# Levels of a chunked recurrence: keys and queries in one row, and three visits to TensorE instead of one per level

## The chip, the cores and the metric

The kernel runs on one core of a Trainium2 chip. The metric is the device time of one execution in microseconds (us). Names of engines as in the profile: PE is TensorE (PEld its weight loads), DVE is VectorE, ACT is ScalarE, POOL is GpSimd, SP is SyncE.

## What is computed

One layer of a hybrid decoder for 2048 prompt tokens and 64 sample tokens (8 sequences of 8), model width 1024. A projection of the normalised input gives nine parts of 1024 columns. Three of them (q, f, v) feed a recurrence with 8 heads of 128 x 128 state; the others feed a convolution branch and gates. Cut to the recurrence, which the change touches:

```python
f = lb + (1.0 - lb) * jax.nn.sigmoid(fz)
k = 1.0 - f
# per token: S_t = diag(f_t) S_{t-1} + (1 - f_t) i_t^T ; o_t = S_t^T q_t, done in chunks:
b = jnp.cumsum(log_f, axis=-2)
decay = jnp.exp(jnp.where(mask, b[..., :, None, :] - b[..., None, :, :], -jnp.inf))
attn = jnp.einsum('bhtk,bhsk,bhtsk->bhts', qc, kc, decay)
o = einsum(attn, v) + einsum(q * exp(b), S)
```

Everything else (projection, gates, convolution, layer norm, output projections) is the same before and after the change.

## The kernel before

**Phases.** The first and longest phase, to about 1960 us, is the projection. It goes over two halves of the tokens (1024 each; the second half also holds the 64 sample tokens) and, in each, over 8 heads. For a head, nine blocks of weights (f, q, v, za, zb, gb, ga, ma, mb) meet each stretch of tokens. One block times one stretch is a *unit*: 24 matmuls into one PSUM bank (line 1356; high and low parts of weights and activations, 8 steps of the contraction, 3 products). A unit of 512 tokens counts as 1.0 on the planner's clock. The first half has units of 512 tokens; the second has 512, 256 and 320. After the projection come the two branch products with the layer norm, and then the output projections (line 1187).

**What hangs between the units.** Everything else of the phase is put into a list with a due time (`at_time`), and the main loop (lines 1338 to 1364) emits, after the 24 matmuls of a unit, all steps whose due time falls into it, in order of priority and time, and then the unit's evacuation. So on PE the small matmuls of the recurrence stand between two units, together with any others due in the same unit. On the page I call such a gap a *visit*. Each engine executes its own list in order.

**The recurrence.** `Hgrn` handles one head and one stretch of 512 tokens (the last stretch also the 64 sample tokens): 8 heads x 4 stretches = 32 instances. The causal 128 x 128 products are built in levels h = 1, 2, 4, 8, 16, 32, 64. At level h, tokens are taken in blocks of 2h; the queries of the second half of a block meet the keys of the first half. `decay(h)` (DVE, line 429) multiplies keys and queries by the running decay and writes them to a level tile; `grow(h)` (line 419) doubles the running decay; `mm_level(h)` (PE, lines 455 and 463) does the products; `mm_diag` (line 441) does the diagonal. Up to level 16 the weights are 32 tokens wide, the output goes to four groups of 32 partitions, and a mask keeps what belongs to the level; level 32 also uses weights of 32 columns, level 64 of 64. All other matmuls of the phase (projection, transposes, `mm_kv`, `mm_o`) use weights of 128 columns. The diagonal and levels 1 to 8 go to the PSUM tile `d32p`, 16 to 64 to `ab`. DVE takes the diagonal and levels 1 to 16 out by `evac_diag` and `evac_level` (lines 470, 479), `final` (line 500) scales keys and queries to the stretch's end, ACT's `gather` copies the blocks into `at`, and `k_turn`, `mm_kv`, `chain`, `mm_o`, `norm_o` and `turn_o` finish.

**The level tiles.** There are three, `lvl[0]` to `lvl[2]`, of two rows of 576. A level uses one tile: row 0 for keys, row 1 for queries, each only at the positions of its half blocks. Level h uses tile `h.bit_length() % 3`, so that a tile comes again every third level.

**Due times.** `plan` (line 614) gives each step its time after the start of the instance. Before the change, decay and grow of the i-th level are due at 0.75 i, its matmuls 1.25 units later (`MMD`), that is at 1.25, 2.0, 2.75, 3.5, 4.25, 5.0 and 5.75; the diagonal at 1.25. The second instance of a head starts 6.1 units or more after the first.

Of the kernel before, what the change touches and what calls it, by code (L numbers as in the profile page):

```python
# [17 lines left out]
P = 128  # L18
# [11 lines left out]
RAW_LAG = 1  # L30
KTS = 7.7
SIN = 1.0
MMD = 1.25
VEC_AT = 6
FILL_PRIO = 0
LNT = (-0.4, 2, 2.6, 4, 5, 8, 8.1, 9.6, 9.1, 10.5)
# [38 lines left out]
def view(t, off, dims):  # L75
    return bass.AP(t.tensor, t.offset + off, [list(t.ap[0])] + [list(d) for d in dims])
# [7 lines left out]
def tile_hybrid_step(  # L84
# [201 lines left out]
    lvl = [c1.tile([P, 2, 576], F32, name=f"lvl{i}") for i in range(3)]  # L286
# [62 lines left out]
    def at_time(t, fn, prio=2):  # L349
        todo.append((t, prio, len(todo), fn))  # L350


    s_state = {}

    class Hgrn:


# [61 lines left out]
            nc.vector.tensor_tensor(out=io, in0=io, in1=tt, op=ALU.mult)  # L419

        def decay(self, h):
            n = self.n if h <= 4 else 512
            nb = n // (2 * h)
            lv = lvl[h.bit_length() % 3]
            if h == 1:
                o, a, b = (view(t, 577, [[2, n // 2]]) for t in (lv, self.kq, self.rp))
            else:
                o, a, b = (view(t, 0, [[576 + h, 2], [2 * h, nb], [1, h]]) for t in (lv, self.kq, self.rp))
            nc.vector.tensor_tensor(out=o, in0=a, in1=b, op=ALU.mult)  # L429

        def chunks(self, h):
# [11 lines left out]
                        start=True, stop=True)  # L443

        def mm_level(self, h):
            lv = lvl[h.bit_length() % 3]
            kk = self.kq if h == 1 else lv
            if h == 16:
                self.ab = ps_1.tile([P, 4, P], F32, tag="ab", name="ab")
            if h <= 16:  # L450
                dst, s = (self.ab, 0) if h == 16 else (d32p, 16 + 16 * h.bit_length())
                for c, nq in self.chunks(h):
                    for b in range(nq):
                        o = P * c + 32 * b
                        nc.tensor.matmul(  # L455
                            dst[32 * b:32 * b + 32, c, s:s + 16], lhsT=kk[:, 0, o:o + 32],
                            rhs=lv[:, 1, o:o + 32].rearrange("p (a e i) -> p a e i", e=2, i=h)[:, :, 1, :],
                            start=True, stop=True)
            else:
                for c in range(4):  # L460
                    for b in range(64 // h):
                        o = 2 * h * b
                        nc.tensor.matmul(
                            self.ab[o:o + h, c, o + h:o + 2 * h], lhsT=lv[:, 0, P * c + o:P * c + o + h],
                            rhs=lv[:, 1, P * c + o + h:P * c + o + 2 * h], start=True, stop=True)

        def evac_diag(self):
            m = self.m
# [145 lines left out]
        def plan(self, t0, tv):  # L614

            smp = self.smp
            ev = []

            def put(t, *fns):
                for fn in fns:  # L620
                    at_time(t0 + t, fn, 0)

            put(0.0, self.prep)
            put(MMD, self.mm_diag)
            for i, h in enumerate((1, 2, 4, 8, 16, 32, 64)):
                put(0.75 * i, lambda h=h: self.decay(h), lambda h=h: self.grow(h))
                put(0.75 * i + MMD, lambda h=h: self.mm_level(h))
            put(3.2, self.evac_diag, lambda: self.evac_level(1), lambda: self.evac_level(2))
            put(4.5, lambda: self.evac_level(4), lambda: self.evac_level(8))
            put(5.25, self.final)  # L630
            put(4.6 + MMD, lambda: self.evac_level(16))
            put(6.25, self.k_turn)
            put(6.6, self.gather)
            put(7.25, self.mm_kv)
            put(8.2, self.chain)
            put(9.0, self.mm_o)
            put(9.9, self.norm_o)
            put(11.2, self.turn_o)
            if smp:
                put(KTS, self.k_turn_sample)  # L640
                put(7.5, self.sample_o)
                put(8.3, self.sample_norm)
                put(9.5, self.sample_turn)
                put(8.0, self.sample_decay)
                put(9.2, lambda: self.sample_state(0))
                put(9.9, lambda: self.sample_state(1))
            at_time(tv, self.v_turn)
            if self.smp:
                at_time(tv + 1.0, self.v_turn_sample)
# [263 lines left out]
    for which, w, times, ev in (("a", w_br_a, t_a, evac_a), ("b", w_br_b, t_b, evac_b)):  # L913
        for hf in range(2):
# [3 lines left out]
            for dms in ((0, 1), (2,), (3,), (4,), (5,), (6, 7)):  # L918
                bs = [Block(w[0][:, P * dm:P * (dm + 1)]) for dm in dms]
                for s in range(2):  # L920
                    for dm, b in zip(dms, bs):
                        for _, t0, c0, n in (p for p in parts if p[0] == s):
                            pre, e = ev(dm, t0, n)
# [142 lines left out]
    for i in range(9):  # L1066
        t, b = XOUT0 + XOUT_STEP * i, 8 + i
# [255 lines left out]
    for t, prio, n, fn in todo:  # L1323
        i = min(bisect.bisect_right(clock, t + 1e-6) - 1, len(units) - 1)
# [5 lines left out]
    for b in range(1, len(blocks)):  # L1330
        i = 1 if b == 2 else max(uses[b][0] - 3, 0)
        if b >= 3:
            i = max(i, min(uses[b - 3][-1] + 1, uses[b][0] - 1))
# [4 lines left out]
    for i, u in enumerate(units):  # L1338
# [13 lines left out]
        for k in range(KB):  # L1352
            for fn in u.mid.get(k, []):
                fn()
            for w, x in ((u.block.hi, xh), (u.block.hi, xl), (u.block.lo, xh)):
                nc.tensor.matmul(  # L1356
                    ps[:, 0:u.n], lhsT=w[:, k, :], rhs=x[:, k, sl],
                    start=(k == 0 and w is u.block.hi and x is xh), stop=(k == KB - 1 and w is u.block.lo))
# [106 lines left out]
```

## Time and profile before

| what | value |
|---|---|
| median of 3 runs | 2814.08 us (2813.54 to 2814.91) |
| the profiled execution | 2815.03 us, of which the profile's span is 2813.2 |
| mean granted clock of PE | 0.996 |
| PE, PEld, DVE, ACT, POOL busy | 2781.4, 2378.6, 1934.6, 932.1, 278.6 us |
| narrow matmuls of the levels (lines 441, 455, 463), records | 1056, 5216, 768 |
| DVE's taps of the convolution (line 696) | 722.4 us in 960 instructions |

A row of a timeline has the start in us from the span's start, the length in us, the engine, the source line, the operation, output<-inputs by the program's names, shapes, and how many alike were merged; behind it, in brackets, the idle time of the engine ahead of it and what ended it. For a matmul the first shape is that of the weights ("128*32": 128 rows, 32 columns), the second that of what streams. Every matmul in plain 32 bits leaves two records; those of the projection leave one. A row of waits reads: engine, what waited <- what for: us in total, number of times, longest. A row of stretches has the stretch, its length, busy us and instructions (x) of PE, PEld, DVE, ACT and POOL, the granted clock, the share of the DMA engines and GB/s. A row of groups ends in busy us, mean ns of one | idle us ahead of it and what ended that.

### The profile page before, as it was taken

What the parts mean: (1) busy time and instruction counts of PE and PEld (TensorE: products, weight loads), DVE (VectorE), ACT (ScalarE), POOL (GpSimd) and SP (SyncE); (2) the same over time, 40 slices, a digit from 0 to 9 for tenths busy, and PEclk for the clock granted to TensorE, in tenths of its full rate; (3) what the DMA queues carried; (4) which work ended last, traced back from release to release, by engine and by line L of the source; (5) the groups of instructions that cost most, each with busy time, mean ns of one, the idle gap of its engine ahead of it and who ended that gap; (6) DMA issues with size and microseconds to landing.
All of it is one profiled execution on the core that took longest, in us unless ns stands there. A gap on an engine that the chain in (4) does not pass through costs nothing. (4 is left out here: it accounts for less than half of the span.)

```text
span 2813.2 us, 50692 instructions
## 1 busy us (share of the span) xinstructions
PE 2781.4 (99%) x21199; PEld 2378.6 (85%) x21199; DVE 1934.6 (69%) x3242; ACT 932.1 (33%) x2119; POOL 278.6 (10%) x441
## 2 busy tenths in 40 slices
PE   8999999999999999999999999999999999999998
PEld 6888888888888888889888888888889789788887
DVE  6577777777778787676777777687977775433433
ACT  5333333333323432323322323233345443322222
POOL 2001000000000000000000000000036420000000
PEclk9999999999999999999999999999999999999999
DMA  3122222222221322122222212223686779422321
GB/s 123 61 72 79 76 81 84 88 83 72 72 68 61 126 62 88 57 73 70 72 63 78 73 61 77 60 85 98 197 279 214 249 254 295 138 87 78 87 84 40
DMA packets 352797, 292.68 MB, mean 104 GB/s; under 512 B 17514, under 2 KB 301259, under 8 KB 352568
## 3 DMA queue, kind: packets, MB, share of 16 engines
q1 hardware_dynamic: 293856, 218.40, 25.7%
q10 hardware_dynamic: 58440, 70.86, 7.4%
q8 instruction: 166, 2.72, 0.4%
q14 instruction: 63, 0.52, 0.1%
q0 software_dynamic: 272, 0.19, 0.0%
HBM read 201.25 MB, written 88.14 MB: 103 GB/s over the span
## 5 line engine op out<-in xcount | busy, mean ns | idle before, releaser
L696 DVE SCALAR_TENSOR_TENSOR acc<-u,cw,acc 128x512 f32<-128x512 f32 x960 | 722.4, 753 | 20.7
L1356 PE MATMUL mm<-x1h,whi 128*128 128x320 f32 (+2 forms) x2112 | 709.6, 336 | 0.0
L1356 PE MATMUL mm<-x1h,wlo 128*128 128x320 f32 (+2 forms) x2112 | 691.3, 327 | 0.0
L1356 PE MATMUL mm<-x1l,whi 128*128 128x320 f32 (+2 forms) x2112 | 690.7, 327 | 0.0
L1356 PE MATMUL mm<-x0h,whi 128*128 128x512 f32 (+1 forms) x1416 | 565.5, 399 | 2.3 <-ACT x0h L1030 1.9
L1356 PE MATMUL mm<-x0l,whi 128*128 128x512 f32 (+1 forms) x1416 | 552.2, 390 | 1.2 <-DVE x0l L176 1.0
L1356 PE MATMUL mm<-x0h,wlo 128*128 128x512 f32 (+1 forms) x1416 | 552.3, 390 | 0.0
L1356 PEld LDWEIGHTS mm<-x1h,whi 128*128 128x128 f32 x2112 | 399.3, 189 | 33.6 <-ACT rp L372 3.8
L1356 PEld LDWEIGHTS mm<-x1h,wlo 128*128 128x128 f32 x2112 | 398.9, 189 | 28.5
L1356 PEld LDWEIGHTS mm<-x1l,whi 128*128 128x128 f32 x2112 | 399.7, 189 | 26.3
L327 DVE TENSOR_TENSOR wlo<-raw,whi 128x1024 fp32r<-128x1024 f32 x176 | 216.5, 1231 | 206.4 <-ACT whi L326 200.3
L1356 PEld LDWEIGHTS mm<-x0h,whi 128*128 128x128 f32 x1416 | 267.3, 189 | 60.2 <-ACT sp L779 2.6
L1356 PEld LDWEIGHTS mm<-x0h,wlo 128*128 128x128 f32 x1416 | 267.2, 189 | 56.8 <-DVE wlo L327 0.4
L1356 PEld LDWEIGHTS mm<-x0l,whi 128*128 128x128 f32 x1416 | 267.6, 189 | 52.6 <-DVE x0l L176 1.2
L326 ACT ACTIVATE whi<-raw 128x1024 fp32r<-128x1024 f32 x176 | 186.0, 1057 | 71.9 <-DVE mal L888 25.3
L1187 PE MATMUL ps<-woh,mgi 128*128 128x512 f32 x528 | 169.5, 395 | 2.5 <-DMA mgi<-mg_dr 2.5
L419 DVE TENSOR_TENSOR rp<-rp 128x512 f32<-128x512 f32 (+1 forms) x224 | 156.7, 700 | 9.6
L429 DVE TENSOR_TENSOR lvl<-kq,rp 128x512 f32<-128x512 f32 (+2 forms) x224 | 146.6, 655 | 23.6 <-PE d32p L455 21.8
L1187 PEld LDWEIGHTS ps<-woh,mgi 128*128 128x128 f32 x528 | 99.9, 189 | 23.4 <-DMA mgi<-mg_dr 2.7
L779 ACT ACTIVATE sp<-mm,vcol 128x512 f32<-128x512 f32 (+2 forms) x120 | 73.1, 609 | 126.9 <-PE mm L1356 113.5
L1261 DVE TENSOR_TENSOR g<-ps,g 128x512 f32<-128x512 f32 x32 | 22.1, 691 | 133.4 <-ACT g L1260 128.6
L560 POOL TENSOR_SCALAR ors<-oss 128x4 f32<-128x4 f32 (+1 forms) x40 | 11.7, 293 | 994.2 <-ACT on L558 994.2
(253 smaller groups left out, 3276.8 us busy)
## 6 DMA issues: line engine op xcount, KB each, us to landing
raw<-in_w_in_dram SPq DMA_DIRECT2D x144, 512.0 KB, 3.9
mgi<-mg_dr SPq DMA_DIRECT2D x16, 1024.0 KB, 6.1
gate<-am_dr SPq DMA_DIRECT2D x24, 512.0 KB, 5.3
mg_dr<-mg SPq DMA_DIRECT2D x24, 512.0 KB, 3.4
xt<-in_x_prompt_dram SPq DMA_DIRECT2D x16, 512.0 KB, 4.9
g_dr<-gst ACTq DMA_DIRECT2D x32, 256.0 KB, 2.7
cv_dr<-acc ACTq DMA_DIRECT2D x32, 256.0 KB, 2.2
raw<-in_w_br_a_dram SPq DMA_DIRECT2D x16, 512.0 KB, 5.3
```

The costliest lines, as they stand in the source:

```text
L326: nc.scalar.activation(out=b.hi, in_=b.raw, func=AF.Copy)
L327: nc.vector.tensor_tensor(out=b.lo, in0=b.raw, in1=f32(b.hi), op=ALU.subtract)
L419: nc.vector.tensor_tensor(out=io, in0=io, in1=tt, op=ALU.mult)
L429: nc.vector.tensor_tensor(out=o, in0=a, in1=b, op=ALU.mult)
L560: nc.gpsimd.tensor_scalar(out=rs[0:n, 0:m], in0=ss[0:n, 0:m], scalar1=1.0 / P, scalar2=EPS, op0=ALU.mult, op1=ALU.add)
L696: nc.vector.scalar_tensor_tensor(out=self.acc, in0=self.u[:, i:i + G], scalar=w, in1=self.acc, op0=ALU.mult, op1=ALU.add)
L779: nc.scalar.activation(out=s[:, 0:n], in_=ps[:, 0:n], func=func, bias=bias(kind, j))
L1187: nc.tensor.matmul(ps, lhsT=a[:, k, :], rhs=c[:, k, s], start=(k == 0 and i == 0), stop=(k == kn - 1 and i == len(ops) - 1))
L1261: nc.vector.tensor_tensor(out=g[0:n], in0=pp[0:n], in1=g[0:n], op=ALU.mult)
L1356: nc.tensor.matmul(ps[:, 0:u.n], lhsT=w[:, k, :], rhs=x[:, k, sl], start=(k == 0 and w is u.block.hi and x is xh), stop=(k == KB - 1 and w ...
```

## The change

Three edits. First, keys and queries of a level go into one row, each at its own positions, and the three tiles serve as six rows, taken by `lvl_row`; only level 64 shares its row with level 1. A narrow matmul of levels 2 to 16 now loads 32 columns in which keys and queries alternate, and the mask keeps the same products as before; level 1 still takes its keys from `kq`. Second, a table `LVT` replaces the delay `MMD`: the diagonal and levels 1 and 2 at 2.0, levels 4, 8 and 16 at 4.25, levels 32 and 64 at 5.4. Third, times that follow: the evacuation of 4 and 8 from 4.5 to 4.9, `k_turn` from 6.25 to 6.35, `mm_kv` from 7.25 to 7.3; the evacuation of 16 stays at 5.85.

```diff
-MMD = 1.25
+LVT = ((2.0, (1, 2)), (4.25, (4, 8, 16)), (5.4, (32, 64)))
...
+    def lvl_row(h):
+        i = (h.bit_length() - 1) % 6
+        return lvl[i // 2][:, i % 2, :]
...
         def decay(self, h):
             n = self.n if h <= 4 else 512
             nb = n // (2 * h)
-            lv = lvl[h.bit_length() % 3]
+            lv = lvl_row(h)
             if h == 1:
-                o, a, b = (view(t, 577, [[2, n // 2]]) for t in (lv, self.kq, self.rp))
+                o = view(lv, 1, [[2, n // 2]])
+                a, b = (view(t, 577, [[2, n // 2]]) for t in (self.kq, self.rp))
             else:
-                o, a, b = (view(t, 0, [[576 + h, 2], [2 * h, nb], [1, h]]) for t in (lv, self.kq, self.rp))
+                o = view(lv, 0, [[h, 2], [2 * h, nb], [1, h]])
+                a, b = (view(t, 0, [[576 + h, 2], [2 * h, nb], [1, h]]) for t in (self.kq, self.rp))
             nc.vector.tensor_tensor(out=o, in0=a, in1=b, op=ALU.mult)
...
         def mm_level(self, h):
-            lv = lvl[h.bit_length() % 3]
-            kk = self.kq if h == 1 else lv
+            lv = lvl_row(h)
+            kk = self.kq[:, 0, :] if h == 1 else lv
...
-                            dst[32 * b:32 * b + 32, c, s:s + 16], lhsT=kk[:, 0, o:o + 32],
-                            rhs=lv[:, 1, o:o + 32].rearrange("p (a e i) -> p a e i", e=2, i=h)[:, :, 1, :],
+                            dst[32 * b:32 * b + 32, c, s:s + 16], lhsT=kk[:, o:o + 32],
+                            rhs=lv[:, o:o + 32].rearrange("p (a e i) -> p a e i", e=2, i=h)[:, :, 1, :],
...
-            put(MMD, self.mm_diag)
             for i, h in enumerate((1, 2, 4, 8, 16, 32, 64)):
                 put(0.75 * i, lambda h=h: self.decay(h), lambda h=h: self.grow(h))
-                put(0.75 * i + MMD, lambda h=h: self.mm_level(h))
+            for t, hs in LVT:
+                put(t, *([self.mm_diag] if 1 in hs else []), *(lambda h=h: self.mm_level(h) for h in hs))
             put(3.2, self.evac_diag, lambda: self.evac_level(1), lambda: self.evac_level(2))
-            put(4.5, lambda: self.evac_level(4), lambda: self.evac_level(8))
+            put(4.9, lambda: self.evac_level(4), lambda: self.evac_level(8))
             put(5.25, self.final)
-            put(4.6 + MMD, lambda: self.evac_level(16))
-            put(6.25, self.k_turn)
+            put(5.85, lambda: self.evac_level(16))
+            put(6.35, self.k_turn)
             put(6.6, self.gather)
-            put(7.25, self.mm_kv)
+            put(7.3, self.mm_kv)
```

How that moves the instructions is seen on two engines. First PE, in one instance of the first half (the second one of a head), before the change. `lvl_143` to `lvl_145` are the three level tiles, and "..." stands for the 24 projection matmuls of a unit or for other small matmuls. An x16 here is 32 records in the trace.

```order
L522 MATMUL kv<-v,kt 128x128 x4
L441 MATMUL d32p<-kq 32x32 x16
L455 MATMUL d32p<-lvl_144,kq 32x16 x16
...
L455 MATMUL d32p<-lvl_145 32x16 x16
L455 MATMUL d32p<-lvl_143 32x16 x16
...
L455 MATMUL d32p<-lvl_144 32x16 x16
...
L455 MATMUL ab<-lvl_145 32x16 x16
...
L463 MATMUL ab<-lvl_143 32x32 x8
L575 MATMUL otr<-ident,on 128x128 x4
L463 MATMUL ab<-lvl_144 64x64 x4
```

And the same instance after it (line numbers are 7 higher from `decay` on).

```order
L529 MATMUL kv<-v,kt 128x128 x4
...
L448 MATMUL d32p<-kq 32x32 x16
L462 MATMUL d32p<-lvl_143,kq 32x16 x16
L462 MATMUL d32p<-lvl_143 32x16 x16
...
L462 MATMUL d32p<-lvl_144 32x16 x32
L462 MATMUL ab<-lvl_145 32x16 x16
...
L582 MATMUL otr<-ident,on 128x128 x4
L470 MATMUL ab<-lvl_145 32x32 x8
L470 MATMUL ab<-lvl_143 64x64 x4
```

Six stretches of narrow matmuls, counting level 64's apart, have become three; the wide ones (kv, the transpose `otr`) are no longer between or beside them in the same way. Second DVE, in the first instance of a head of the second half, before the change, with what each row waits for, from the decay of level 64 to the evacuation of level 16.

```order
L429 TENSOR_TENSOR lvl_144<-kq,rp 128x2x4x64 [waits PE_49]
L419 TENSOR_TENSOR rp<-rp 128x2x4x64 [waits DVE_49]
L479 COPY_PREDICATED d_15890<-lmask_140,d32p 128x16x4
L479 COPY_PREDICATED d_15890<-lmask_141,d32p 128x8x8 [waits DVE_49]
L696 SCALAR_TENSOR_TENSOR acc<-u,cw,acc 128x512
L500 TENSOR_TENSOR kq<-kq,rp 128x2x512
```

And after it.

```order
L436 TENSOR_TENSOR lvl_143<-kq,rp 128x2x4x64
L423 TENSOR_TENSOR rp<-rp 128x2x4x64 [waits DVE_49]
L703 SCALAR_TENSOR_TENSOR acc<-u,cw,acc 128x512
L486 COPY_PREDICATED d_15874<-lmask_140,d32p 128x16x4 [waits PE_49]
L486 COPY_PREDICATED d_15874<-lmask_141,d32p 128x8x8 [waits DVE_49]
L507 TENSOR_TENSOR kq<-kq,rp 128x2x512
```

The decay of level 64 has lost its wait for PE, and the evacuation of level 4 has gained one and stands one tap of the convolution later.

More of the change, by code (lines that the diff above doesn't have):

```diff
@@ L463, in mm_level @@
                         nc.tensor.matmul(
-                            self.ab[o:o + h, c, o + h:o + 2 * h], lhsT=lv[:, 0, P * c + o:P * c + o + h],
-                            rhs=lv[:, 1, P * c + o + h:P * c + o + 2 * h], start=True, stop=True)
+                            self.ab[o:o + h, c, o + h:o + 2 * h], lhsT=lv[:, P * c + o:P * c + o + h],
+                            rhs=lv[:, P * c + o + h:P * c + o + 2 * h], start=True, stop=True)
         def evac_diag(self):
```

## The prediction

> **What bounds the kernel now.** I read the page's totals first, then the busy time by stretches.
>
> ```profile
> span 2813.2 us, 50692 instructions
> PE 2781.4 (99%) x21199; PEld 2378.6 (85%) x21199; DVE 1934.6 (69%) x3242; ACT 932.1 (33%) x2119; POOL 278.6 (10%) x441
> 40.00:1000.00 960.00, 960.00 (x7977) 791.96 (x7975) 705.86 (x1081) 320.32 (x674) 49.11 (x75) 1.00 0.25 77
> 1000.00:1960.00 960.00, 960.00 (x8936) 853.89 (x8936) 716.01 (x1237) 292.14 (x683) 60.95 (x73) 1.00 0.23 70
> ```
>
> The last two rows (length, then busy us of PE, PEld, DVE, ACT and POOL, then clock) cover the projection stage with all 32 instances of the recurrence. PE is busy for all 960 us of each at a granted clock of 1.00; DVE, next of the engines that compute, has 705.86 and 716.01, about 74%. So whatever PE is spared there leaves the span, unless another engine comes late. The list of PE's waits says who has been late so far:
>
> ```profile
> PE xtr L172 <- DVE xt L160: 11.8, 3, 9.8
> PE rs L1009 <- POOL diag L1001: 5.2, 2, 4.8
> ```
>
> These are the longest two in the whole run, and they lie at the start and in the layer-norm phase. For 40 to 1960 us the same view lists no wait of PE at all. A busy PE is not a PE at its peak, though: the records overlap, and what counts is how far apart they start. I therefore went to PE's timeline and measured each visit of small matmuls from the start of the last projection matmul before it to the start of the second one after it.
>
> ```profile
> 679.24 0.39 PE L1356 MATMUL mm<-x0l,whi 128*128 128x512 f32 x1
> 679.47 0.39 PE L1356 MATMUL mm<-x0h,wlo 128*128 128x512 f32 x1
> 679.79 0.73 PE L455 MATMUL d32p<-lvl 128*32 128x16 f32 x64
> 680.45 0.50 PE L1356 MATMUL mm<-x1h,whi 128*128 128x512 f32 x1
> 680.79 0.39 PE L1356 MATMUL mm<-x1l,whi 128*128 128x512 f32 x1
> ...
> 693.79 0.39 PE L1356 MATMUL mm<-x1h,wlo 128*128 128x512 f32 x1
> 694.11 0.45 PE L455 MATMUL ab<-lvl 128*32 128x16 f32 x32
> 694.49 0.50 PE L1356 MATMUL mm<-x0h,whi 128*128 128x512 f32 x1
> 694.82 0.39 PE L1356 MATMUL mm<-x0l,whi 128*128 128x512 f32 x1
> ```
>
> Undisturbed, one projection matmul starts 0.23 us after the other (679.24 to 679.47; 0.227 over a whole unit). The visit with 64 narrow records (weights 32 columns wide, "128*32"; a 32-bit matmul leaves two records) takes 680.79 - 679.47 = 1.32, less two undisturbed steps of 0.227: 0.866 us. The visit with 32 takes 1.03, less 0.454: 0.576. So 32 more records in the same visit cost 0.290 us, 9 ns each, and a visit with none would still cost 0.576 - 0.290 = 0.286. It can be seen where this lies: the matmul ahead of the visit holds PE 0.32 instead of 0.23, the first one after it 0.33 or 0.34, and the last narrow record a little. I call it the price of changing the width of the weights twice, 128 to 32 and back: 0.143 us a change.
>
> The second question is whether the price belongs to the visit or to the width. A visit with wide small matmuls alone (kv), and one in which the same kv is followed by narrow ones:
>
> ```profile
> 713.01 0.40 PE L1356 MATMUL mm<-x0h,wlo 128*128 128x512 f32 x1
> 713.25 1.05 PE L522 MATMUL kv<-v,kt 128*128 128x128 f32 x8
> 714.06 0.48 PE L1356 MATMUL mm<-x1h,whi 128*128 128x512 f32 x1
> 714.37 0.40 PE L1356 MATMUL mm<-x1l,whi 128*128 128x512 f32 x1
> ...
> 787.99 0.40 PE L1356 MATMUL mm<-x0h,wlo 128*128 128x512 f32 x1
> 788.22 1.06 PE L522 MATMUL kv<-v,kt 128*128 128x128 f32 x8
> 789.21 0.46 PE L441 MATMUL d32p<-kq 128*32 128x32 f32 x32
> 789.48 0.47 PE L455 MATMUL d32p<-lvl,kq 128*32 128x16 f32 x32
> 789.89 0.50 PE L1356 MATMUL mm<-x0h,whi 128*128 128x512 f32 x1
> 790.22 0.40 PE L1356 MATMUL mm<-x0l,whi 128*128 128x512 f32 x1
> ```
>
> kv alone costs 1.36 - 0.454 = 0.906. kv with 64 narrow records costs 2.23 - 0.454 = 1.776, or 0.870 more, and 64 narrow records in a visit of their own cost 0.866. Sharing a visit with wide matmuls spares nothing; only narrow beside narrow does. What has to be counted is changes of width.
>
> **The change, part by part.**
>
> *Visits.* The number of matmuls and their sizes stay. In the order of PE's instructions I counted places where the weight width changes among 128 (projections, transposes, kv, o), 32 (diagonal, levels 1 to 32) and 64 (level 64). Before: 11 or 12 per instance in the first half, 12 or 14 in the second, 392 in all. After: two for the first visit, two for the second, three for the third (128, 32, 64, 128): 7 x 32 = 224. That is 168 fewer, 144 of them at stretches of 32 (168 stretches become 96, two ends each), 24 at stretches of 64, which now always follow level 32. 168 x 0.143 = 24.0 us off PE's path.
>
> For the 24 no quoted row gives a price by itself; its ends are 0 and 0.143, the latter being the nearest row of a width change, and I take that one. With 0 the sum is 20.6. [...]
>
> *Wide groups left alone.* k_turn, kv, o and v_turn shared 113 borders with narrow groups and now share 36. By the rows above sharing is worth -0.004 us, with the last digits good for ±0.02, so the loss is between 0 and 77 x 0.02 = 1.5. I take 0.8. Sum: 24.0 - 0.8 = 23.2.
>
> *Rows of keys and queries.* DVE's decay writes as many elements in as many instructions.
>
> ```profile
> L429 DVE TENSOR_TENSOR lvl<-kq,rp 128x512 f32<-128x512 f32 (+2 forms) x224 | 146.6, 655 | 23.6 <-PE d32p L455 21.8
> ...
> DVE lvl L429 <- PE d32p L455: 21.8, 21, 4.0
> DVE d L479 <- PE ab L463: 125.7, 22, 10.1
> ```
>
> Only its output address differs, so I cost it at nothing; bounds are ±10% of 146.6 us on DVE, which some 245 us of idle in each stretch cover. With six rows instead of three, a decay no longer waits for the level three before it: up to 21.8 us of DVE's idle time goes. That is worth nothing to the span, since PE waits for no decay. The weights of a level now hold queries between the keys; they are still 32 columns, and the extra products fall where the masks don't select.
>
> *Waits added.* Levels 4 and 8 now run after level 16's old time, while DVE's evacuation of both (L479) stays nearly in its place. At one instance of the second half:
>
> ```profile
> 1126.02 0.48 DVE L479 COPY_PREDICATED d<-lmask,d32p 128x64 f32<-128x64 int32 x2
> 1126.41 0.75 DVE L696 SCALAR_TENSOR_TENSOR acc<-u,cw,acc 128x512 f32<-128x512 f32 x1
> 1127.07 1.22 DVE L500 TENSOR_TENSOR kq<-kq,rp 128x1024 f32<-128x1024 f32 x1
> ...
> 1138.89 0.23 DVE L479 COPY_PREDICATED d<-lmask,ab 128x64 f32<-128x64 int32 x1 [9.94 <-PE ab L463]
> ...
> 1128.00 0.45 PE L455 MATMUL ab<-lvl 128*32 128x16 f32 x32
> 1128.43 0.39 PE L1356 MATMUL mm<-x1h,whi 128*128 128x320 f32 x1
> ```
>
> DVE would reach the evacuation, now one tap later, at about 1127.1. The new visit stands on PE where level 16 stood (1128.00) and is 64 records longer, so it ends at about 1129.0: a new wait of some 2.0 us. Behind it on DVE stand `final` (k_turn needs it), taps and the splits of weights that the projections need. I cost it at nothing: a few instructions later the same queue waits 9.94 us for level 64 anyway, 125.7 us over 22 such places, and PE shows no wait for it. If that cover were gone, 2.0 us at each of the 16 first instances of a head would be 32 us.
>
> *Moved earlier.* Level 64 goes from 5.75 to 5.4 units after the start. At eight instances of the second half that is one visit sooner: right behind level 32's present place. Here are one of six that are alike and the last, which is the tightest: each time the decay of level 64 on DVE, then level 32 on PE.
>
> ```profile
> 1171.84 0.68 DVE L429 TENSOR_TENSOR lvl<-kq,rp 128x512 f32<-128x512 f32 x1
> ...
> 1175.52 0.45 PE L463 MATMUL ab<-lvl 128*32 128x32 f32 x16
> ...
> 1948.85 0.68 DVE L429 TENSOR_TENSOR lvl<-kq,rp 128x512 f32<-128x512 f32 x1
> ...
> 1950.95 0.45 PE L463 MATMUL ab<-lvl 128*32 128x32 f32 x16
> ```
>
> The decay ends 3.0 us ahead of PE at the one and 1.4 us at the last, so PE should not wait; without that margin it would cost about a DVE instruction, 0.7 us, at each of the eight, 5.6 us. k_turn and kv move by 0.1 and 0.05 units later, towards less waiting.
>
> **Against which time.** The profiled execution took 2815.03 us (span 2813.2); 2815.03 - 23.2 = 2791.8. It is 0.95 above the median of the runs, 2814.08, and the gain is the same, so for the median I forecast 2814.08 - 23.2 = 2790.9, given as 2791.
>
> **Rivals.**
>
> *The price belongs to the visit, not the width.* Visits of any small matmul fall only from 341 to 318. 23 x 0.286 = 6.6: 2807.5. For it: each visit does show a longer first projection matmul behind it, kv's too (0.31). Against: the kv rows, where two groups in one visit cost the sum of both. Chance 0.05.
>
> *The price belongs to the single matmul, and there is no gain.* [...] As a mechanism here: a fixed time for each narrow record, whose number doesn't change, so 2814. Against it the rows have 9 ns a record and 0.286 that doesn't grow with the number. Chance 0.03.
>
> *Slower: the new wait of DVE reaches PE.* Evacuations of levels 4 and 8 hold DVE's queue, a weight split behind them comes late, and the next projection block waits. Price 32 us at 16 places: 2814.1 - 23.2 + 32 = 2822.9. It decides once DVE's later wait for level 64 is shorter than the new one. For it: DVE is 74% busy and executes in order. Against: the 9.94 behind it, and that DVE is the one that waits for PE. Chance 0.04.
>
> **How the numbers follow.** Forecast 0.88, rivals 0.05, 0.03, 0.04. The price is 0.143 ± 0.013 from the last digits of the four starts (21.8 to 26.2 us); with a loss of 0 to 1.5 and the 24 changes at 0 the gain is 17 to 26 us: 2788 to 2797. I widen it to 2787 to 2799: above for part of the 5.6 us at level 64, below for the 1.4 us by which runs differ (2813.54 to 2814.91). A measurement can tell about 0.2% (5.6 us) from no change. Faster by more: 0.88 and most of the first rival, 0.92; same 0.045; slower 0.035.
>
> **What would show it.** Right: the same count of narrow records, a visit of diagonal, 1 and 2 costing about 0.286 + 96 x 0.009 = 1.15 us, starts of 0.32 and 0.33 around only three visits an instance, no PE wait between 40 and 1930 us, fewer DVE waits at L429's place, some new ones of about 2 us at the evacuation of level 4. Wrong: PE waits on DVE's or ACT's weight splits or on a decay, more than 9 ns a record in the long visits, or single wide visits that cost more than 0.9 (kv).

## The result, and the profile after

The changed kernel takes 2790.52 us (median of 4 runs, 2788.37 to 2791.38) against 2813.81 before: 23.3 us less, a ratio of 0.9915 (95% interval 0.9902 to 0.9928). The forecast was 2791 with 2787 to 2799.

The totals of the page after, and its stretches (columns as before):

```profile
span 2786.6 us, 50684 instructions
PE 2754.3 (99%) x21199; PEld 2371.3 (85%) x21199; DVE 1943.8 (70%) x3242; ACT 931.4 (33%) x2119; POOL 283.4 (10%) x441
...
40.00:1000.00 960.00, 960.00 (x8048) 799.89 (x8047) 713.79 (x1093) 325.51 (x687) 50.17 (x76) 1.00 0.25 78
1000.00:1960.00 960.00, 960.00 (x9031) 864.06 (x9030) 739.91 (x1263) 298.72 (x700) 66.44 (x75) 1.00 0.25 75
```

PE does the same 21199 matmuls and is still busy throughout both stretches; it just gets through more of them there (8048 and 9031 against 7977 and 8936). Busy time alone would not have shown a gain. The three new visits of one instance of the first half:

```profile
671.02 0.39 PE L1363 MATMUL mm<-x0h,wlo 128*128 128x512 f32 x1
671.33 0.46 PE L448 MATMUL d32p<-kq 128*32 128x32 f32 x32
...
672.28 0.50 PE L1363 MATMUL mm<-x1h,whi 128*128 128x512 f32 x1
672.62 0.40 PE L1363 MATMUL mm<-x1l,whi 128*128 128x512 f32 x1
...
685.12 0.39 PE L1363 MATMUL mm<-x1h,wlo 128*128 128x512 f32 x1
685.44 0.70 PE L462 MATMUL d32p<-lvl 128*32 128x16 f32 x62
...
686.37 0.50 PE L1363 MATMUL mm<-x0h,whi 128*128 128x512 f32 x1
686.71 0.40 PE L1363 MATMUL mm<-x0l,whi 128*128 128x512 f32 x1
...
691.74 0.39 PE L1363 MATMUL mm<-x0h,wlo 128*128 128x512 f32 x1
691.98 0.60 PE L582 MATMUL otr<-ident,on 128*128 128x128 f32 x4
692.50 1.05 PE L470 MATMUL ab<-lvl 128*32 128x32 f32 x24
693.49 0.50 PE L1363 MATMUL mm<-x1h,whi 128*128 128x512 f32 x1
693.82 0.39 PE L1363 MATMUL mm<-x1l,whi 128*128 128x512 f32 x1
```

Read as in the prediction (start to start, less 0.454): the first visit, diagonal with 1 and 2, costs 672.62 - 671.02 - 0.454 = 1.146 us, where 1.15 was forecast; the second, also 96 records, 1.136. Where the 23 us came off is seen in the last of the 32 `mm_o` steps, which ends the recurrence and kept its due time. Records of the two lines, shortest, median and longest ns, then first and last start; before, then after:

```profile
L549 PE MATMUL o<-v,at x256: 270/275/377, 102.2 to 1978.3; 128*128 128x128 f32 x128
```

```profile
L556 PE MATMUL o<-v,at x256: 270/275/275, 100.5 to 1953.9; 128*128 128x128 f32 x128
```

It stands 1.7 us earlier in the first instance and 24.4 in the last. The remaining 2.2 of the 26.6 by which the two spans differ come later, where both kernels have the same work, and nothing shown ties them to the change; the profiled execution after was the fastest of its four.

Who waits now, on PE and on DVE, after (line numbers 7 higher):

```profile
PE xtr L172 <- DVE xt L160: 11.7, 4, 9.2
PE rs L1016 <- POOL diag L1008: 5.3, 2, 4.9
...
DVE d L486 <- PE ab L470: 84.4, 15, 6.5
...
DVE d L486 <- PE d32p L462: 27.6, 13, 7.1
...
L436 DVE TENSOR_TENSOR lvl<-kq,rp 128x512 f32<-128x512 f32 (+2 forms) x224 | 146.6, 655 | 1.9
```

PE's long waits are the two of before, and between 40 and 1960 us it again has none. The decay is as long as it was (655 ns) and no longer waits for a free tile (idle 1.9 instead of 23.6). The evacuation of levels 4 and 8 has the new wait, 27.6 us in 13 places, and the wait that follows it for level 64 fell by more, from 125.7 to 84.4. So DVE now waits for part of that time one step earlier.

### The profile page after: what moved, and what is told of

It is laid out like the page before. It is cut to its first block, busy times and chain, and to the rows that moved or that the text cites. A ratio compares the mean times of both kernels' runs of the same rounds, so it can differ in the third digit from the quotient of the medians.

```text
span 2786.6 us, 50684 instructions
## 1 busy us (share of the span) xinstructions
PE 2754.3 (99%) x21199; PEld 2371.3 (85%) x21199; DVE 1943.8 (70%) x3242; ACT 931.4 (33%) x2119; POOL 283.4 (10%) x441
## 3 DMA queue, kind: packets, MB, share of 16 engines
q8 instruction: 166, 2.72, 0.4%
## 5 line engine op out<-in xcount | busy, mean ns | idle before, releaser
L703 DVE SCALAR_TENSOR_TENSOR acc<-u,cw,acc 128x512 f32<-128x512 f32 x960 | 734.1, 765 | 20.7
```

The costliest lines, as they stand in the source:

```text
L703: nc.vector.scalar_tensor_tensor(out=self.acc, in0=self.u[:, i:i + G], scalar=w, in1=self.acc, op0=ALU.mult, op1=ALU.add)
```

## The experiments

Each is an edit of the changed kernel, timed against the kernel before on the same chip (2813.6 to 2814.1 us there).

**The rows alone.** Old due times, new rows:

```diff
-            for t, hs in LVT:
-                put(t, ...)
+            put(1.25, self.mm_diag)
+            for i, h in enumerate((1, 2, 4, 8, 16, 32, 64)):
+                put(0.75 * i + 1.25, lambda h=h: self.mm_level(h))
```

> Only the rows: keys and queries of a level in one row, six rows in use, but the diagonal and the seven levels at their old times (1.25 and 0.75 apart), evacuations, k_turn and mm_kv too. Width theory (what costs is each change of the weights' width on TensorE): 392 changes and 341 visits as before, so no change, 2813.8 us within 2, though DVE's 21.8 us of waits for a free level tile go. Rival (the rows themselves speed up DVE and with it PE): up to 21.8 us, down to 2792.

Measured: 2814.05 us, ratio 1.0 (0.9991 to 1.0009). The rows by themselves gain nothing; they only make the grouping possible. DVE's 21.8 us of waits for a free tile were worth nothing to the span.

**Same visits, more changes of width.** The third visit alternates:

```diff
+        def mm_wide(self):
+            for c in range(4):
+                for h in (32, 64):
...
+            put(5.4, self.mm_wide)
```

> The changed kernel, but in the third visit the matmuls of levels 32 and 64 alternate (two of 32 columns, one of 64, four times) instead of standing one level after the other. Same matmuls, same 318 visits; width changes go from 224 to 416. Width theory at 0.14 us a change: 192 x 0.14 = 27 us more than the changed kernel, about 2817, slower than before by 3. Visit theory: no change from the changed kernel, 2790.5. If a change between 32 and 64 columns costs less than one to 128: in between.

Measured: 2815.90 us, ratio 1.0004 (0.9995 to 1.0014): 25.4 us slower than the changed kernel for 192 more changes, 0.132 us each. All of the gain is gone with the number of visits as it was. The rows show the same on one visit, of the alternating kernel and then of the kernel before (each with the wide `xtr` behind it):

```profile
543.71 1.84 PE L480 MATMUL ab<-lvl 128*32 128x32 f32 x24
545.49 0.66 PE L188 MATMUL xtr<-ident,xt 128*128 128x128 f32 x4
```

```profile
543.43 1.05 PE L463 MATMUL ab<-lvl 128*32 128x32 f32 x24
544.42 0.65 PE L188 MATMUL xtr<-ident,xt 128*128 128x128 f32 x4
```

From the first of the 24 records to the transpose it is 1.78 us against 0.99: 0.79 more for 6 further changes, 0.132 each. These further changes are all between 32 and 64 columns, so such a change costs about what one to 128 does (0.143 in the rows before).

**More visits, same changes of width.** kv and o in two halves, the second one inside the next unit:

```diff
+            self.mm_kv_part((0, 1))
+            self.kv_rest = self.rest(lambda: self.mm_kv_part((2, 3)))
...
+            self.mm_o_part((0, 1))
+            self.o_rest = self.rest(lambda: self.mm_o_part((2, 3)))
```

> The changed kernel, but kv and o (weights of 128 columns) are cut in two: the second two of four blocks of tokens come inside the next unit, after four of its eight steps. Same matmuls, same 224 width changes, visits from 318 to 382. Width theory: at most 0.5 us more, 2791. Visit theory at 0.286 us a visit: 64 x 0.286 = 18.3 us more, about 2809.

Measured: 2793.01 us, ratio 0.9927 (0.9913 to 0.994). 64 more visits cost 2.5 us, a seventh of the 18.3 that the visit theory asks, but more than the 0.5 expected. PE's waits between 40 and 1960 us show where most of it lies:

```profile
PE mm L1383 <- DVE x0l L205: 1.4, 1, 1.4
PE vtr L395 <- DVE gst L604: 1.2, 1, 1.2
```

The changed kernel has no wait there at all; these two, between 940 and 966 us, make 2.6 us. Comparing the starts of the same projection matmuls in the two profiled executions, the halves fall behind by 0.7 us up to 940 us, by 3.3 us from there to 966 and by 0.3 us from 966 to 1947 us. Outside that place it is 1.0 us in all, 0.016 for each further visit. Why DVE is late there is not shown.

**Two visits, the early ones joined.**

```diff
-LVT = ((2.0, (1, 2)), (4.25, (4, 8, 16)), (5.4, (32, 64)))
+LVT = ((4.25, (1, 2, 4, 8, 16)), (5.4, (32, 64)))
-            put(3.2, self.evac_diag, ...
+            put(4.85, self.evac_diag, ...
```

> The changed kernel with its first two visits joined: diagonal and levels 1 to 16 at 4.25, 32 and 64 at 5.4; evacuation of the diagonal and levels 1 and 2 from 3.2 to 4.85. Width changes from 224 to 160. Width theory: 64 x 0.14 = 9 us less, about 2781.5. Rival (DVE's waits reach PE): the decay of level 64 shares its row with level 1 and must now wait for the joined visit, up to a unit of 5.4 us in each of 32 instances, and so PE waits for it in the second visit where units are short: no gain, or slower than 2790.

Measured: 2817.22 us, ratio 1.0012 (1.0003 to 1.0021): 26.7 us slower than the changed kernel, with 64 fewer changes. DVE did wait for the shared row, as the rival has it. PE did stand still too, but almost all of it for nothing that the profile names ("issue"; one wait for DVE, of 1.0 us, comes beside it):

```profile
DVE lvl L436 <- PE d32p L462: 114.7, 24, 8.4
...
PE ab L462 <- issue: 13.1, 6, 2.7
PE d32p L462 <- issue: 7.4, 6, 2.1
PE mm L1363 <- issue: 4.2, 3, 1.9
```

**The same without the shared row.** The visits stay joined, but level 64 gets a tile of its own, so that DVE's wait goes:

```diff
+            if h == 64:
+                self.l64 = h1.tile([P, 4, P], F32, tag="kt", name="l64")
```

> The two joined visits once more, but level 64 has a row of its own (a tile that the later copy of k uses anyway), so its decay no longer waits for level 1. Width changes 160, as in the kernel with the shared row. If that wait of DVE (114.7 us in 24 places) was what cost 26 us there: TensorE's waits inside the joined visit go, and the time falls to what the widths say, 2790.5 - 64 x 0.14 = 2781.5. If long visits cost by themselves (more narrow matmuls in one stretch, or evacuations that come late): it stays near 2817.

Measured: 2814.78 us, ratio 1.0005 (0.9996 to 1.0014). My theory for the slow joined visits fell: that wait of DVE is off its list, and PE stands still as before. Its timeline, waits and stretches there:

```profile
415.32 0.85 PE L466 MATMUL d32p<-lvl 128*32 128x16 f32 x80
418.73 0.22 PE L466 MATMUL d32p<-lvl 128*32 128x16 f32 x3 [2.55 <-issue]
...
PE ab L466 <- issue: 12.9, 6, 2.3
PE d32p L466 <- issue: 8.0, 6, 2.6
PE mm L1367 <- issue: 4.7, 4, 1.9
...
412.00:415.00 3.00, 3.00 (x50) 2.26 (x49) 1.37 (x3) 0.22 (x1) 0.00 (x0) 1.00 0.00 0
415.00:419.00 4.00, 1.45 (x172) 1.34 (x160) 0.00 (x0) 1.41 (x2) 0.00 (x0) 1.00 0.01 4
419.00:421.00 2.00, 2.00 (x34) 1.63 (x22) 1.91 (x5) 0.00 (x0) 0.00 (x0) 0.77 0.03 8
421.00:423.00 2.00, 2.00 (x6) 1.51 (x6) 1.93 (x4) 0.00 (x0) 0.00 (x0) 0.50 0.34 100
423.00:426.00 3.00, 3.00 (x14) 2.46 (x13) 1.78 (x4) 0.00 (x0) 0.00 (x0) 0.92 0.36 108
```

PE stops for 2.55 us in the middle of the narrow stretch. A little later the granted clock, the third number from the end, goes to 0.50 and back, which costs another 0.23 x 2 + 0.50 x 2 + 0.08 x 3 = 1.7 us. Seven of the 12 stops of over 1 us are followed by such a fall, the other five are not. I then counted PE's matmul records between one of these 12 and the next: 384, 1532, 384, 2932, 765, 1659, 765, 1148, 1660, 764 and 1659: multiples of 127.75 in every case, to within 0.05 of a multiple. The page's queue of kind "instruction" moves 166 packets:

```profile
q8 instruction: 166, 2.72, 0.4%
```

2.72 MB in 166 are 16.4 KB each, and PE's 21199 matmuls divided by 166 are 127.7 to a packet, the spacing of the stops (with as many weight loads, 255 instructions). In the trace a packet of this queue, 0.9 to 1.4 us long, starts between 2.3 and 2.7 us before each of the 12 stops ends, whether the stop is 1.0 or 2.55 us long. From these numbers I formed a theory, the instruction theory below: PE stands there for the next packet, or block, because 128 narrow records, at 9 ns each, take only 1.15 us, where 128 projection matmuls take 29. No view shows that PE waits for the packet.

**One visit.** Everything at 5.4, `final` and the evacuations behind it, level 64 again with a tile of its own:

```diff
+LVT = ((5.4, (1, 2, 4, 8, 16, 32, 64)),)
+            put(5.45, self.final)
+            put(5.85, self.evac_diag, *(lambda h=h: self.evac_level(h) for h in (1, 2, 4, 8, 16)))
```

> All levels and the diagonal in a single visit at 5.4, level 64 with a row of its own, final after it, all evacuations at 5.85. Width changes 96 (128, 32, 64, 128 in each instance). Width theory: 128 x 0.14 = 18 us less than the changed kernel, 2772.5. If DVE's late run of evacuations and final reaches TensorE (k_turn needs final one unit later): 2775 to 2795, with waits of TensorE at the transposes of k or at a decay.

Measured: 2832.07 us, ratio 1.0062 (1.0046 to 1.0078), slower than anything expected. PE's waits there, and one of the stops:

```profile
PE ab L466 <- issue: 19.4, 9, 2.6
...
PE d32p L466 <- issue: 10.6, 7, 2.2
PE ab L474 <- issue: 9.9, 5, 2.5
...
74.38 0.32 PE L466 MATMUL ab<-lvl 128*32 128x16 f32 x16
76.72 0.28 PE L466 MATMUL ab<-lvl 128*32 128x16 f32 x11 [2.03 <-issue]
```

20 stops of over 1 us, again at multiples of 128 records, none of them a wait for DVE.

**Two visits, the late ones joined.**

```diff
+LVT = ((2.0, (1, 2)), (5.4, (4, 8, 16, 32, 64)))
-            put(4.9, lambda: self.evac_level(4), lambda: self.evac_level(8))
-            put(5.85, lambda: self.evac_level(16))
+            put(5.85, *(lambda h=h: self.evac_level(h) for h in (4, 8, 16)))
```

> Two visits joined the other way: diagonal, 1 and 2 at 2.0, levels 4 to 64 together at 5.4, evacuation of 4, 8 and 16 together at 5.85; the shared row stays, and no decay has to wait. Width changes 160. Width theory: 64 x 0.14 = 9 us less than the changed kernel, 2781.5, with no wait of TensorE inside the visits. If DVE's evacuation, now all behind the late visit, holds up what follows: 2785 to 2795.

Measured: 2782.94 us, ratio 0.9888 (0.9874 to 0.9901): the widths' forecast, 1.4 us off. Its narrow stretches have 96 and 120 records (108 and 124 with the sample tokens), and no PE wait of the kind "issue" is left between 40 and 1960 us. The last `mm_o` of its profiled execution, for the comparison below:

```profile
L556 PE MATMUL o<-v,at x256: 270/275/275, 100.6 to 1944.9; 128*128 128x128 f32 x128
```

**Length of the narrow stretch.** If that theory holds, what counts is how many records stand in a stretch, not which. Two kernels, joined at level 4 and at level 8, each with the evacuations moved behind its visits:

```diff
+LVT = ((2.75, (1, 2, 4)), (5.4, (8, 16, 32, 64)))
...
+LVT = ((3.5, (1, 2, 4, 8)), (5.4, (16, 32, 64)))
```

> Two visits: diagonal, 1, 2 and 4 at 2.75; 8 to 64 at 5.4. 160 width changes. The longest narrow stretch has 128 records (144 with the sample tokens). Instruction theory (TensorE runs dry when the edge of a 16 KB block of instructions, 128 records, falls late in a long narrow stretch; in the joined visits of 192 records no stall came before the 142nd): no stall or one, so 2782 us, as with the other join. Rival (it is the diagonal and low levels coming late, with their evacuation, that costs): slower than the changed kernel, between 2795 and 2815.

> Two visits: diagonal, 1, 2, 4 and 8 at 3.5; 16 to 64 at 5.4. 160 width changes. The first stretch has 160 records (176 with the sample tokens). Instruction theory: an edge falls beyond the 142nd record in (160 - 142) / 128 of 24 instances and (176 - 142) / 128 of 8, about 5.5 stalls of some 2 us with a low clock behind each, against 12 in the visits of 192: about 2782 + 5.5/12 x 32 = 2797. Rival (late low levels): as slow as the joined visits before, near 2815. If neither holds: 2782.

Measured: 2783.78 us, ratio 0.9886 (0.9872 to 0.9899), and 2798.11 us, ratio 0.9941 (0.9927 to 0.9954). PE's stops between 40 and 1960 us, joined at 4 and then at 8:

```profile
PE d32p L462 <- issue: 0.8, 1, 0.8
PE mm L1363 <- issue: 0.4, 1, 0.4
```

```profile
PE d32p L462 <- issue: 10.0, 8, 2.7
PE mm L1363 <- issue: 3.7, 3, 1.5
```

Against the other join (2782.94) the 160 records cost 15.2 us by the medians. In the profiled executions it can be seen where. The join at 8, its last `mm_o` and its two stretches of low clock:

```profile
L556 PE MATMUL o<-v,at x256: 270/275/275, 99.4 to 1962.0; 128*128 128x128 f32 x128
...
1410.00:1414.00 4.00, 4.00 (x22) 4.00 (x21) 2.92 (x4) 0.12 (x2) 0.00 (x0) 0.57 0.37 107
1884.00:1888.00 4.00, 4.00 (x25) 4.00 (x22) 3.14 (x7) 1.18 (x2) 0.00 (x0) 0.57 0.02 4
```

The last `mm_o` starts 17.1 us later than in the other join (1962.0 against 1944.9). The stops are 13.7 us, and a clock of 0.57 over 4 us costs 1.7 us each time: 17.1 together. In the joined visits of 192 records without the shared row (the profiled execution, the slowest of its 11) it is 25.6 us of stops and seven falls of the clock, 37.5 together, where the last `mm_o` stands 39.2 us later (1984.1). So at most some 2 us are left for low levels coming late, and the join at 4, where they come later too, shows no such cost.

## Why the prediction was right

- *PE's starts set the stage.* Held. PE waits for nothing from 40 to 1960 us before and after, and the last `mm_o` moved by 24.4 us.
- *The price of a change of width, 0.143 us, by 168.* Held. 24.0 was forecast for the stage; 24.4 less the 0.5 us by which this execution's first projection matmul already started earlier is 23.9, or 0.142 a change. The alternating kernel gives 0.132 in the other direction. The late join spares 64 more: 7.6 us by the medians, 0.119 each, and 9.4 by the last `mm_o` (9.0 earlier, though its first projection matmul started 0.4 later), 0.147. As a rule for a next step, 0.12 to 0.15.
- *The 24 changes at level 64, taken at the full price.* Held. The price had been taken from the nearest row, as an estimate; the alternating kernel changes between 32 and 64 and pays 0.132 us a change, against 0.142 over all 168. What PE does in that time is not shown.
- *Wide groups left alone, 0.8 us.* Too small to be told: the stage gained 23.9, against 24.0 before this loss is taken off and 23.2 with it, and the ±0.013 of the price alone is ±2.2 us. By the halves experiment a wide visit of its own costs about 0.016 us; for the 77 lost borders that would be 1.2 us, of the size assumed. The runs after the change differ by 3.0 us, so that the measured 23.3 meets 23.2 to 0.1 us is luck; that it lies near 24 is not.
- *Rows at nothing, DVE's lost waits at nothing.* Held: the rows alone give 2814.05.
- *The new wait at the evacuation of levels 4 and 8, at nothing.* Held: it came to 27.6 us at 13 places (2.0 at each of 16 had been worked out), the wait behind it fell by 41.3, and PE waited for neither. The slower rival is not refuted as a mechanism; in this kernel its point was not reached.
- *Level 64 one visit sooner.* No wait of PE appeared.
- *The visit theory* (0.05) is refuted twice, by more changes of width in as many visits and by more visits with as many changes. *A fixed cost per matmul* (0.03) would have left 2814.

What the prediction did not see is the limit behind the next step: it took long visits to cost 9 ns a record and nothing else. That held in the late join, with up to 124 records in a stretch (1.4 us off the forecast), and no longer with 160 (15.2 us more than the late join).

## What to carry to other kernels

When PE is busy throughout, look at the distance between starts around each small visit, and count changes of the weights' width, not visits: placing matmuls of one width side by side spared 0.12 to 0.15 us a change here, and placing them beside wide ones spared nothing (64 narrow records cost 0.870 us behind kv, 0.866 alone). Group only up to a length at which PE shows no stop: the best version found joins levels 4 to 64 (or 1 to 4) and takes 2782.94 us, while 160 records in one stretch lose part of the gain and 192 all of it. Before blaming the engine that waits, remove its wait alone; here PE's stops stayed (24.7 us with that wait of DVE, 25.6 without).

## What had not been expected of the hardware

PE stopped for 1 to 2.7 us at multiples of about 128 matmul records (127.75 where I counted between the stops), never before the 142nd record of a narrow stretch in the joined visits of 192 (the join at 4 shows one shorter stop, of 0.8 us, at the 125th of a stretch of 144). The granted clock fell to 0.50 behind a stop of 2.55 us, as it did behind six more of the 12 stops of that run. The packets of the queue "instruction" have 16.4 KB, and there is one for every 127.7 matmuls of the run. No stop came with at most 124 narrow records in a row, but 12 of over 1 us in the run with stretches of 192. That PE waits there for such a packet is my conclusion, not shown: it rests on the spacing of the stops, on the packets' times and on the forecast for 160 records (2797 against 2798.11, though with 7 stops of over 1 us where 5.5 had been worked out); no view names the cause. Why the limit lies between 124 and some 140 records, and why the clock fell behind some stops and not behind others, stays open.
